# A norm between two layers done token tile by token tile in a held order, latent rows copied out of PSUM, and two attention heads taken two to a step

## The chip, the cores and the metric

The kernel runs on one core of a Trainium2 chip. The metric is the device time of one execution in microseconds, the median of several runs. Engines are named as the profile names them: PE (TensorE matmul), PEld (its weight load), DVE (VectorE), ACT (ScalarE), POOL (GpSimd) and SP (SyncE, which issues nearly all DMA transfers).

## The reference

256 tokens of width 2048 go through one gated-MLP layer and one attention layer, all in float32. Cut to what matters:

```
x:   256 tokens x 2048          c: a vector of 2048 (conditioning)
mod  = silu(c) @ W_ada + b      # shift, scale, gate (2048 each) for layer a, layer b; shift, scale for the shared keys

# layer a (gated MLP)
h        = rms_norm(x, g0) * (1 + scale_a) + shift_a
u, v, z  = split(h @ w_in)                       # 2048 -> 3 x 4096
v        = layer_norm(gelu(v));  mixed = per group of 256 columns: tril(w_s) @ v + b_s
x1       = x + gate_a * ((gelu(u) * mixed * silu(z)) @ w_out)          # 4096 -> 2048

# shared keys and values, from x1
c_kv, k_r = split(mod_k(rms_norm(x1)) @ w_dkv)   # 512 and 64 columns
c_kv = rms_norm(c_kv);  k_nope, v = heads(c_kv @ w_ukv);  k_rope = rope(rms_norm(k_r))

# layer b (attention, 16 heads)
h        = rms_norm(x1, g1) * (1 + scale_b) + shift_b
c_q, z   = split(h @ w_in)                       # 512 and 2048 columns
q        = heads(rms_norm(c_q) @ w_uq);  o = causal_attention(q, k, v)
out      = x1 + gate_b * ((o * silu(z)) @ w_out)
```

## The kernel before

**Tiling.** The tokens are two tiles of 128 (`t` = 0, 1). A product is a `Block`: 1024 output columns (two PSUM banks of 512 for each tile, `pm` in the profile), over k-steps of 256 rows of the weight. Each k-step streams 1 MB of weights (`load`, tile `raw`). A float32 product is made of three reduced-precision ones: ACT casts the weights to `hi` (L192), DVE takes the remainder `lo` (L197), the activations are split likewise (`hh`/`hl` in the input blocks, `shi`/`slo` in the first out-projection and the dkv block, `gh`/`gl` for the second norm, `ybh`/`ybl` in the last projection), and PE does hi·hi, lo·hi and hi·lo: 24 matmuls of 128x512 a k-step for the two tiles and two banks (L392).

**Background work.** The modulation vectors need 128 further loads of 1 MB (`araw`, L214) and one DVE product each (L222; the last gate `ga1` in four pieces of 512, L222 `part`). They are spread over the k-steps by quotas: `AQ` a step in layer a, `BQ` in the z blocks, `OQ` in the last projection. `STOP = 14` ends them at k-step 14 of the second a_w_out block. `raw` and `araw` share a ring of four buffers, `hi` and `lo` rings hold two k-steps, and large intermediates sit in 13 slots of `big`.

**Order.** Work is written as items with a `prepare` (load and split), a `compute` (matmuls) and a `post`; `drive` (L396 on) prepares the next item before it computes the present one, and pops one function from the list `later` (an attention head, a transposed latent row) after each. SP's order is the written one. On PE, ACT and DVE a scheduler orders what is ready, except where `nc.keep("order")` pins an engine's written order and where `behind(...)` puts one instruction after another.

**Second norm.** The second a_w_out block (k-steps 0 to 15) has `TAIL = 1`: its last k-step is done tile by tile, each tile followed by its two residuals (L707 product with the gate, L708 sum, DVE) and, for each, `norm1.chunk`: the sum of squares (L173, ACT) and four transposes (L293, PE; copied to `zT` by ACT, L295). Then `early1(t)` takes the reciprocal root (L186, L167 on DVE, L168 on POOL), spreads it over the partitions with a PE transpose (`px<-ident,rs`, L323), scales the first `EARLY = 4` rows of `zT` (L332, DVE) and makes the first four h (L340 and L341 on ACT, L350 on DVE: tiles `h`, `gh`, `gl`). `late1` does the other twelve for both tiles together. The z block (`b_w_z`, matmuls `pm<-hi,gh` and so on) reads them.

**Latent rows.** After the dkv block and after the q block, `latent_row` sums the squares straight from PSUM (L173), takes the reciprocal root and scales from PSUM to `cn` (L800). Only then are the banks free for the next block.

**Out-projection.** The two b_w_out blocks start while the last heads are still in `later`; each half of the last gate is collected at k-step `GATE1` = 3 (first block) and 4 (second block), and loads whatever `ga1` products are still missing.

**Start.** `opening` splits the first weights, makes the first two h, and runs two pairs of modulation products on DVE in a pinned order (`nc.keep("order")`, all under L69).

Of the kernel before, what the change touches and what calls it, by code (L numbers as in the profile page):

```python
# [10 lines left out]
F32R = mybir.dt.float32r  # L11
# [34 lines left out]
STOP = 14  # L46
# [69 lines left out]
def trunk_kernel(ctx: ExitStack, tc: tile.TileContext, a: dict, out: bass.AP):  # L116
# [74 lines left out]
    def split(src, hi, lo):  # L191
        nc.scalar.copy(hi, src)  # L192
        with behind(chain.pop(0) if chain and queue[0] else None):
            rest(src, hi, lo)
# [8 lines left out]
    hold, queue, chain = [None], [False], []  # L203
# [75 lines left out]
    class Norm:  # L279
# [10 lines left out]
        def flip(self, t, q):  # L290
            p = bank("px")
            for j in range(4):
                nc.tensor.transpose(p[:, j * P:(j + 1) * P], self.xt[t][:, (q * 4 + j) * P:(q * 4 + j + 1) * P], ident)  # L293
            dst = self.ts[q // 2].rearrange("p (k t) -> p k t", t=S)[:, (q % 2) * 4:(q % 2) * 4 + 4, t * P:(t + 1) * P]
            nc.scalar.copy(dst, p.rearrange("p (k t) -> p k t", t=P))  # L295
# [41 lines left out]
        def high(self, n, k, hi, t0=0, t1=S):  # L337
# [5 lines left out]

        def part(self, k, dst):

            src = self.ts[k // 8][:, (k % 8) * S:(k % 8 + 1) * S]
            nc.scalar.activation(dst, src, AF.Identity, scale=ada["sc0"].col[:, k:k + 1], bias=ada["sh0"].col[:, k:k + 1])
# [35 lines left out]
    def mms(ps, t, lh, wt, widths, first, last, apart=False):  # L383

        offs = [sum(widths[:i]) for i in range(len(widths))]
        for some in ([[i] for i in range(len(widths))] if apart else [range(len(widths))]):
# [11 lines left out]
    def drive(items):  # L398
# [5 lines left out]
        while nxt:  # L404
# [3 lines left out]
            if nxt and not late:  # L408
                queue[0] = True
                ready = nxt[0]()  # L410
                queue[0] = False
            cur[1](got)
            if nxt and late:
                queue[0] = True
                ready = nxt[0]()
                queue[0] = False
# [4 lines left out]
    class Block:  # L421
# [21 lines left out]
        def close(self, evac=None, t=None):  # L443
            for t_ in range(NT) if t is None else (t,):
                for i, wd in enumerate(self.widths):
# [4 lines left out]
        def items(self, quota=0.0, tail=0, after=None, before=None, then=None, start=0, stop=99, at_step={}):  # L450
            n = self.nkk - tail
            for kk in range(n):
# [8 lines left out]
            if tail:  # L461
# [8 lines left out]
                def comp(got):  # L470
                    for t in range(NT):
# [3 lines left out]
                        if after:  # L475
                            after(t)
                def post():
                    if then:
                        then()
                    bg(quota * tail if n < stop else 0.0)  # L480
                yield (prep, comp, post, "late") if then else (prep, comp, post)
# [93 lines left out]
    def opening(b):  # L575
# [12 lines left out]
        split(raw[:, 1:2, :], *wt[1])  # L588
# [489 lines left out]
```

## Time and profile before

| what | value |
|---|---|
| time, median of 3 runs | 1129.98 us (1128.75 to 1131.89) |
| the profiled execution's own time | 1134.16 us |
| its span | 1132.5 us, mean granted PE clock 0.995 |
| busy share PE / PEld / DVE / ACT / POOL | 97% / 81% / 84% / 55% / 5% |
| matmul and transpose instructions | 5128 |
| DMA | 340.41 MB, mean 301 GB/s |

The page is to be read from two sides. Its shares say that PE works nearly all the time. Its list of waits says where PE does not, and the windows and the timeline say how each such place runs and at which granted clock (`PEclk`). The profiled execution lay 4.2 us above the median of the runs.

### The profile page before, as it was taken

The numbers are of one execution on the slowest core, as the hardware profiler recorded it, in microseconds if no ns is written. First come the engines' busy times: TensorE is split into PE (matmuls) and PEld (weight loads), VectorE is DVE, ScalarE is ACT, GpSimd is POOL, SyncE is SP. The second block draws the span as 40 slices with busy tenths as digits, with TensorE's granted clock in tenths as the row PEclk, the third lists the DMA queues.
The fourth block names the chain that finished last, engine by engine and source line by source line (L and its number), as shares of the span: only waits on it lengthen the run. The fifth ranks groups of instructions, "written<-read, shape, count | busy, mean of one in ns | idle before, by whom it ended". The sixth has DMA issues, their size and how long they took to land.

```text
span 1132.5 us, 14354 instructions
## 1 busy us (share of the span) xinstructions
PE 1097.4 (97%) x5128; PEld 912.6 (81%) x5128; DVE 950.4 (84%) x1375; ACT 620.3 (55%) x1146; POOL 62.2 (5%) x79
## 2 busy tenths in 40 slices
PE   5999999999999999999999999989999999999998
PEld 4877788887888887888888888868889788898876
DVE  5889899988997887897798899869877658779985
ACT  6844444456754435435354455457737579885322
POOL 1000000000310000000000000000000024220000
PEclk9999999999999999999999999999999999999999
DMA  9987889887998988989979989967896645245893
GB/s 384 353 342 291 329 330 364 343 311 282 351 338 300 367 327 318 386 305 342 343 297 353 375 335 375 353 234 288 318 341 224 221 152 194 105 166 215 301 343 128
DMA packets 52328, 340.41 MB, mean 301 GB/s; under 512 B 5888, under 2 KB 6304, under 8 KB 13984
## 3 DMA queue, kind: packets, MB, share of 16 engines
q1 hardware_dynamic: 50400, 335.29, 78.7%
q0 software_dynamic: 704, 2.11, 0.6%
q10 hardware_dynamic: 1152, 2.10, 0.5%
q8 instruction: 40, 0.66, 0.2%
q14 instruction: 32, 0.26, 0.1%
HBM read 337.36 MB, written 2.11 MB: 300 GB/s over the span
## 4 chain that ended last, share of the span: by engine, by line
PE 73%; DVE 11%; DMA 9%; ACT 3%; issue 3%; POOL 0%; SPq 0%; DVEq 0%; ACTq 0%; POOLq 0%
PE pm L392 60%; DMA araw<-in_ada_wT 5%; PE pk L392 4%; DVE lo L197 4%; DVE araw L222 3%; PE pq L392 2%; DMA araw<-in_kv_ada_wT 2%; DMA raw<-in_b_w_z 1%; PE pmix L663 1%; ACT hi L192 1%; PE pS L967 1%; PE pS L968 1%; DVE v L537 1%; PE pt L670 1%; DVE araw L69 1%
## 5 line engine op out<-in xcount | busy, mean ns | idle before, releaser
L192 ACT CAST hi<-raw 128x1024 fp32r<-128x1024 f32 (+2 forms) x372 | 376.3, 1029 | 358.6 <-PE pm L392 238.8
L197 DVE TENSOR_TENSOR lo<-raw,hi 128x1024 fp32r<-128x1024 f32 (+2 forms) x372 | 436.9, 1195 | 60.5 <-ACT hi L192 58.0
L222 DVE CUSTOM_DVE_ANT_0 araw<-araw,s_b,vec 128x2048 f32<-128x2048 f32 (+1 forms) x124 | 265.6, 2142 | 55.1 <-DMA araw<-in_ada_wT 48.4
L392 PE MATMUL pm<-lo,hh 128*128 128x512 f32 x760 | 245.2, 392 | 3.0 <-DVE lo L197 2.9
L392 PE MATMUL pm<-hi,hl 128*128 128x512 f32 x760 | 243.6, 391 | 0.0
L392 PE MATMUL pm<-hi,hh 128*128 128x512 f32 x760 | 238.2, 393 | 2.6 <-DVE u L537 1.2
L392 PEld LDWEIGHTS pm<-hi,hh 128*128 128x128 f32 x760 | 142.1, 188 | 35.5 <-ACT hi L192 2.2
L392 PEld LDWEIGHTS pm<-lo,hh 128*128 128x128 f32 x760 | 141.6, 188 | 35.3 <-DVE lo L197 6.4
L392 PEld LDWEIGHTS pm<-hi,hl 128*128 128x128 f32 x760 | 142.5, 188 | 29.8
L392 PE MATMUL pm<-lo,shi 128*128 128x512 f32 (+1 forms) x320 | 95.0, 373 | 0.0
L392 PE MATMUL pm<-hi,slo 128*128 128x512 f32 (+1 forms) x320 | 93.4, 371 | 0.0
L392 PE MATMUL pm<-hi,shi 128*128 128x512 f32 (+1 forms) x320 | 91.3, 373 | 0.6 <-ACT hi L192 0.6
L392 PEld LDWEIGHTS pm<-hi,shi 128*128 128x128 f32 x320 | 58.2, 188 | 11.3 <-ACT hi L192 0.9
L392 PEld LDWEIGHTS pm<-lo,shi 128*128 128x128 f32 x320 | 58.2, 188 | 10.1 <-DVE lo L197 0.6
L392 PEld LDWEIGHTS pm<-hi,slo 128*128 128x128 f32 x320 | 58.0, 188 | 10.1
L392 PE MATMUL pm<-hi,gh 128*128 128x512 f32 x160 | 52.3, 400 | 3.5 <-ACT cn L800 2.3
L392 PE MATMUL pm<-lo,gh 128*128 128x512 f32 x160 | 52.8, 397 | 0.0
L392 PE MATMUL pm<-hi,gl 128*128 128x512 f32 x160 | 52.6, 397 | 0.0
L192 ACT CAST shi<-yT 128x512 fp32r<-128x512 f32 x32 | 19.8, 622 | 46.1 <-PE pm L392 46.0
L392 PE MATMUL pm<-hi,ybh 128*128 128x512 f32 x128 | 42.9, 398 | 1.4 <-ACT ybh L192 1.4
L392 PE MATMUL pm<-hi,ybl 128*128 128x512 f32 x128 | 43.1, 399 | 0.0
L392 PE MATMUL pm<-lo,ybh 128*128 128x512 f32 x128 | 43.0, 394 | 0.0
(207 smaller groups left out, 1282.3 us busy)
## 6 DMA issues: line engine op xcount, KB each, us to landing
araw<-in_ada_wT SPq DMA_DIRECT2D x96, 1024.0 KB, 6.6
raw<-in_a_w_in SPq DMA_DIRECT2D x96, 1024.0 KB, 6.7
raw<-in_a_w_out SPq DMA_DIRECT2D x32, 1024.0 KB, 6.9
araw<-in_kv_ada_wT SPq DMA_DIRECT2D x32, 1024.0 KB, 7.3
raw<-in_b_w_z SPq DMA_DIRECT2D x16, 1024.0 KB, 7.5
raw<-in_b_w_out SPq DMA_DIRECT2D x16, 1024.0 KB, 6.1
raw<-in_kv_w_ukv SPq DMA_DIRECT2D x8, 1024.0 KB, 4.9
raw<-in_b_w_uq SPq DMA_DIRECT2D x8, 768.0 KB, 4.5
```

Source lines behind the costliest of these rows:

```text
L69: ins = f(*args, **kw)
L192: nc.scalar.copy(hi, src)
L197: nc.vector.tensor_tensor(out=lo, in0=src, in1=hi.bitcast(F32), op=ALU.subtract)
L222: nc.vector.tensor_tensor_reduce(out=t[:, c], in0=t[:, c], in1=s_b[:, c], scale=1.0, scalar=acc, op0=ALU.mult, op1=ALU.add, accum_out=dst)
L392: nc.tensor.matmul(ps[i][:, :widths[i]], lhsT=lt, rhs=rhs[:, offs[i]:offs[i] + widths[i]], start=(first and c == 0 and which == 0 and rhs ...
L537: nc.vector.tensor_tensor(out=p, in0=ps, in1=p, op=ALU.add)
L663: nc.tensor.matmul(pmix[:, j * 256:(j + 1) * 256], lhsT=wsh["T"][:, g, :], rhs=piece(vt[i], t, n)[:, j * 256:(j + 1) * 256], start=True, s ...
L670: nc.tensor.transpose(pt[:, j * P:(j + 1) * P], y[:, j * P:(j + 1) * P], ident)
L967: nc.tensor.matmul(pS[:, c0:c1], lhsT=qT[:, j, t * P:(t + 1) * P], rhs=kT[:, j, 0:nk], start=True, stop=False)
L968: nc.tensor.matmul(pS[:, c0:c1], lhsT=qrT[:, t * P:(t + 1) * P], rhs=krT[:, j, 0:nk], start=False, stop=True)
```

## The change

Four places of the program change; the arithmetic is the same but for the place at which a latent row is scaled.

1. `passage()` replaces the last two k-steps of the second a_w_out block and the first two of the first z block by one item whose order is pinned on PE, ACT and DVE: tile 0 through k-steps 14 and 15, its residuals, sums and reciprocal root; tile 1 through both, bank by bank, with the work of tile 0's norm among it; then z k-steps 0 and 1 for tile 0, with tile 1's norm among them; then the same for tile 1. z k-step 0's weights are split into two slots of `big` (`zw`), and sums of squares come right behind each residual, transposes later. `early1`, `chunk`, `finish`, `chain` and `queue` go. `STOP` is 13, and `late1` moves the place behind which background products are held (`hold[0]`) every four h.
2. `latent_row` copies the PSUM banks to SBUF with DVE; a new `normalise` then sums, and scales the copy. The dkv block does its last k-step tile by tile.
3. `onward` pops one more item of `later` at k-steps 1 and 2 of the first b_w_out block.
4. In `opening`, the second `lo` comes behind the second pair of modulation products.

```diff
-STOP = 14
+STOP = 13
...
-        def chunk(self, t, q):
-            self.sums(t, q)
-            self.flip(t, q)
-
-        def finish(self, t):
-
+        def rstd(self, t):
             if self.rb is None:
                 self.rb = const.tile([P, S], F32, name=self.name + "rb")
-            r = rstd_sum(self.st[t], 4, D)
+            return rstd_sum(self.st[t], 4, D)
+
+        def spread(self, r):
+
             p = bank("px")
             nc.tensor.transpose(p[:, :P], r.broadcast_to([P, P]), ident)
             return p[:, :P]
...
         norm0.low(h, h0.at(0, 0), h0.at(1, 0))
-        split(raw[:, 1:2, :], *wt[1])
+        nc.scalar.copy(wt[1][0], raw[:, 1:2, :])
         ada["sh0"].step()
         ada["sc0"].step()
+        rest(raw[:, 1:2, :], *wt[1])
...
-                norm1.chunk(t, 2 * i + n)
+                norm1.sums(t, 2 * i + n)
+                if i == 0:
+                    norm1.flip(t, n)
...
-            yield from b.items(AQ, tail=TAIL, after=early1 if i else None, then=late1 if i else None, before=fetch, stop=STOP if i else 99)
+            if i == 0:
+                yield from b.items(AQ, tail=TAIL, before=fetch)
+            else:
+                yield from b.items(AQ, tail=2, stop=STOP, bare=True)
+                at["z"] = z_block(0)
+                yield passage(b, at["z"], fetch)
+
+    def passage(b, z, fetch):
...
+            nc.keep("order")
+            for c in range(2):
+                s = slot(f"zw{c}", F32R)
+                z0.append((s[:, 0:NB], s[:, NB:2 * NB]))
+                split(begin[:, c], *z0[c])
+            mms(b.ps[0], 0, la, wa, wd, False, False)
+            mms(b.ps[0], 0, lb, wb, wd, False, True, True)
+            b.close(t=0)
+            mms(b.ps[1], 1, la, wa, wd, False, False)
+            mms(b.ps[1], 1, lb, wb, wd, False, True, [0])
+            r = norm1.rstd(0)
+            hi, lo = ([wsp.tile([P, 1, NB], F32R, tag=g, name=g) for _ in range(2)] for g in ("hi", "lo"))
+            z1 = [(hi[c][:, 0, :], lo[c][:, 0, :]) for c in range(2)]
+            for c in range(2):
+                nc.scalar.copy(hi[c], raw[:, c:c + 1, :])
+            rest(raw[:, 0:1, :], hi[0], lo[0])
+            rb = norm1.spread(r)
+            norm1.scale(0, EARLY, 0, P, rb)
+            mms(b.ps[1], 1, lb, wb, wd, False, True, [1])
+            p = norm1.turn(0, 2)
...
+            z.ps = [[bank("pm", "mm") for _ in z.widths] for _ in range(NT)]
+            mms(z.ps[0], 0, z.lhs(0), z0, wd, True, False)
+            p = norm1.turn(0, 3)
+            norm1.flipped(0, 3, p)
+            mms(z.ps[0], 0, z.lhs(1), z1[:1], wd, False, False)
+            r = norm1.rstd(1)
+            rest(raw[:, 1:2, :], hi[1], lo[1])
+            rb = norm1.spread(r)
+            norm1.scale(0, EARLY, P, S, rb)
+            mms(z.ps[0], 0, lambda c, w: z.lhs(1)(1, w), z1[1:], wd, False, False)
+            p = norm1.turn(1, 2)
+            for k0 in range(0, EARLY, 2):
+                hs = [norm1.high("1", k, at1[k][0], P, S) for k in (k0, k0 + 1)]
+                for k in (k0, k0 + 1):
+                    hold[0] = norm1.low(hs[k - k0], *at1[k])
+            norm1.keep(1, rb)
+            norm1.flipped(1, 2, p)
+            for j, w in enumerate((z0, z1)):
+                mms(z.ps[1], 1, z.lhs(j), w, wd, j == 0, False)
+            nc.keep("behind")
+            norm1.flip(1, 3)
+        return prep, comp, late1, "late"
...
-            norm1.h("1", k, h1.at(0, k), h1.at(1, k))
+            low = norm1.h("1", k, h1.at(0, k), h1.at(1, k))
+            if k % 4 == 1:
+                hold[0] = low
...
-        r = rms_rstd(pieces)
         cn = scratch([P, R], "cn", "b")
         o = 0
         for p in pieces:
             n = p.shape[-1]
-            nc.scalar.activation(cn[:, o:o + n], p, AF.Identity, scale=r)
+            nc.vector.tensor_copy(cn[:, o:o + n], p)
             o += n
         return cn
+
+    def normalise(row):
+        nc.scalar.activation(row, row, AF.Identity, scale=rms_rstd([row]))
...
+        def onward():
+            if later:
+                later.popleft()()
...
-            yield from b.items(OQ, tail=1, at_step={GATE1[i]: lambda i=i: gate1.half(i)})
+            yield from b.items(OQ, tail=1, at_step={GATE1[i]: lambda i=i: gate1.half(i), **({1: onward, 2: onward} if i == 0 else {})})
```

On PE, at the end of the second a_w_out block, the program had this order (`shi`, `slo`: the block's activations; `x_0_185`, `x_1_186`: the residual rows of tile 0 and 1; `rs`: a tile's reciprocal root):

```order
L392 MATMUL pm<-hi,slo 128x512
L293 MATMUL px<-ident,x_0_185 128x128 x8
L323 MATMUL px<-ident,rs_5839 128x128
L293 MATMUL px<-ident,x_1_186 128x128 x8
L392 MATMUL pm<-hi,gh_5844 128x512 x2
L392 MATMUL pm<-lo,gh_5844 128x512 x2
L323 MATMUL px<-ident,rs_5901 128x128
L392 MATMUL pm<-hi,gl_5846 128x512 x2
```

It now has this one (what `passage` issues carries the line of the pinned order, L69):

```order
L69 MATMUL px<-ident,rs_5844 128x128
L69 MATMUL pm<-hi,shi 128x512
...
L69 MATMUL px<-ident,x_0_185 128x128 x4
L69 MATMUL pm<-zw_5784,gh_5780 128x512 x4
L69 MATMUL pm<-zw_5784,gl_5782 128x512 x2
L69 MATMUL pm<-zw_5787,gh_5780 128x512 x4
L69 MATMUL pm<-zw_5787,gl_5782 128x512 x2
L69 MATMUL px<-ident,x_0_185 128x128 x4
L69 MATMUL pm<-hi,gh_5780 128x512 x2
L69 MATMUL pm<-lo,gh_5780 128x512 x2
L69 MATMUL pm<-hi,gl_5782 128x512 x2
L69 MATMUL px<-ident,rs_5925 128x128
```

Tile 0's spread moved ahead of the last bank of tile 1, tile 1's behind three quarters of tile 0's share of the two z steps, and the transposes of the residual rows are no longer together. On DVE, a little later, when the other h are made, the order was:

```order
L332 TENSOR_TENSOR zT_188<-zT_188,zrb 128x1024 x2
L222 ISA araw,col_sck<-araw,s_b,vec 128x2048
L222 ISA col_sck 128x1
L197 TENSOR_TENSOR lo<-raw,hi 128x1024
L350 TENSOR_TENSOR gl_5846<-h,gh_5844 128x256 x2
L197 TENSOR_TENSOR lo<-raw,hi 128x1024
L226 SCALAR_TENSOR_TENSOR col_sck<-col_sck,vec 128x1
L197 TENSOR_TENSOR lo<-raw,hi 128x1024 x2
L350 TENSOR_TENSOR gl_5846<-h,gh_5844 128x256 x2
L222 ISA araw,col_shk<-araw,s_b,vec 128x2048
```

and is now:

```order
L353 TENSOR_TENSOR gl_5783<-h,gh_5781 128x256 x2
L221 ISA araw,col_shk<-araw,s_b,vec 128x2048
L221 ISA col_shk 128x1
L221 ISA araw,col_sck<-araw,s_b,vec 128x2048
L221 ISA col_sck 128x1
L221 ISA araw,col_shk<-araw,s_b,vec 128x2048
L221 ISA col_shk 128x1
L353 TENSOR_TENSOR gl_5783<-h,gh_5781 128x256 x2
L196 TENSOR_TENSOR lo<-raw,hi 128x1024
```

Three background products that stood one by one between remainders now stand in a row, behind most of the h. After the dkv block, ACT scaled the latent rows straight out of PSUM:

```order
L173 ACTIVATE sq,ss_6960<-pm 128x288
L173 ACTIVATE sq,ss_6960<-pm 128x224
L192 CAST hi<-raw 128x1024
L800 ACTIVATE cn<-pm,rs_6968 128x288
L800 ACTIVATE cn<-pm,rs_6968 128x224
L173 ACTIVATE sq,ss_6974<-pm 128x64
L843 ACTIVATE kn<-pm,rs_6978 128x64
```

and now DVE takes them out of PSUM, behind two remainders of the next block's weights:

```order
L196 TENSOR_TENSOR lo<-raw,hi 128x1024 x2
L870 COPY cn<-pm 128x288
L870 COPY cn<-pm 128x224
L914 COPY kn<-pm 128x64
L870 COPY cn<-pm 128x288
L870 COPY cn<-pm 128x224
L914 COPY kn<-pm 128x64
L196 TENSOR_TENSOR lo<-raw,hi 128x1024 x2
L167 TENSOR_SCALAR rs_6945<-ss_6942 128x1
```

The root and the scale moved behind the copies. On SP, in the first b_w_out block, the loads around the first half of the last gate were in this order:

```order
L214 DMA araw<-in_ada_wT 128x2048
L367 DMA raw<-in_b_w_out 128x2048
L214 DMA araw<-in_ada_wT 128x2048 x3
L367 DMA raw<-in_b_w_out 128x2048
L214 DMA araw<-in_ada_wT 128x2048
```

and are now in this:

```order
L213 DMA araw<-in_ada_wT 128x2048
L370 DMA raw<-in_b_w_out 128x2048
L213 DMA araw<-in_ada_wT 128x2048 x4
L370 DMA raw<-in_b_w_out 128x2048
L213 DMA araw<-in_ada_wT 128x2048
```

One more modulation load stands ahead of that block's sixth weight load.

More of the change, by code (lines that the diff above doesn't have):

```diff
@@ L192, in split @@
         nc.scalar.copy(hi, src)
-        with behind(chain.pop(0) if chain and queue[0] else None):
-            rest(src, hi, lo)
+        rest(src, hi, lo)
     def rest(src, hi, lo):
@@ L448, in close, with items @@
                 self.ps = None
-        def items(self, quota=0.0, tail=0, after=None, before=None, then=None, start=0, stop=99, at_step={}):
+        def items(self, quota=0.0, tail=0, before=None, start=0, stop=99, skip=0, bare=False, at_step={}):
             n = self.nkk - tail
-            for kk in range(n):
+            for kk in range(skip, n):
                 def post(kk=kk):
@@ L859, in ev_q @@
         cn = latent_row([ps])
+        normalise(cn)
         if t == 0:
```

81 lines of the change are left out of this document (48 added, 33 removed).

## The prediction

> **What bounds the kernel now.** I read the page's shares first, then PE's list of waits, then windows and the timeline round each wait that the change touches.
>
> ```profile
> PE 1097.4 (97%) x5128; PEld 912.6 (81%) x5128; DVE 950.4 (84%) x1375; ACT 620.3 (55%) x1146; POOL 62.2 (5%) x79
> ```
>
> PE works 97% of the span, and the change takes no matmul away. So nothing can be won but what PE loses: some 35 us of idle time (1132.5 - 1097.4), and what its slow stretches add. The list of PE's waits (total, times, longest) names the losses. These are the ones in reach:
>
> ```profile
> PE pm L392 <- ACT cn L800: 2.3, 1, 2.3
> PE px L323 <- POOL rs L168: 2.1, 1, 2.1
> PE pm L392 <- ACT ybh L192: 1.4, 1, 1.4
> PE pm L69 <- ACT hh L69: 1.0, 1, 1.0
> PE pm L392 <- ACT gh L341: 0.8, 1, 0.8
> ```
>
> They sum to 7.6 us, but two of these waits cost more than their length. The windows (length, then busy time of PE, PEld, DVE, ACT, POOL, then granted PE clock, DMA share, GB/s) show it:
>
> ```profile
> 755.60:763.00 7.40, 3.64 (x18) 2.62 (x17) 5.67 (x13) 6.73 (x18) 0.81 (x2) 0.74 0.02 4
> 763.00:767.40 4.40, 4.39 (x14) 3.45 (x15) 3.85 (x7) 3.15 (x11) 0.30 (x1) 0.65 0.24 80
> 767.40:785.00 17.60, 17.60 (x79) 14.53 (x78) 17.60 (x23) 12.63 (x24) 0.00 (x0) 1.00 0.74 282
> 881.60:885.60 4.00, 3.97 (x11) 3.12 (x12) 1.11 (x5) 1.91 (x9) 1.10 (x2) 0.57 0.71 279
> 1075.00:1095.00 20.00, 18.60 (x83) 14.99 (x82) 19.85 (x37) 5.82 (x7) 0.00 (x0) 1.00 0.91 337
> ```
>
> After the norm's wait (755.6 to 763) and after the latent row's (before 881.6) PE is "busy" at a clock of 0.65 and 0.57: 14 and 11 instructions in 4 us, where the third row does 79 in 17.6 us, 0.223 us each. Behind the 1.4 us wait for `ybh` (last row) the clock stayed 1.00.
>
> **The passage into the z block.** The timeline there (start, length, engine):
>
> ```profile
> 667.23 0.60 PE L293 MATMUL px<-ident,x 128*128 128x128 f32 x4
> 667.58 0.71 PE L392 MATMUL pm<-lo,shi 128*128 128x512 f32 x2
> ...
> 755.41 0.39 PE L392 MATMUL pm<-hi,slo 128*128 128x512 f32 x1
> 757.03 0.69 DVE L707 TENSOR_TENSOR x<-pm,gate 128x512 f32<-128x512 f32 x1
> 757.63 1.28 DVE L708 TENSOR_TENSOR x<-x,xr 128x512 f32<-128x512 f32 x2
> 758.15 0.63 ACT L173 ACTIVATE sq<-x 128x512 f32<-128x512 f32 x1
> 758.90 0.16 DVE L186 TENSOR_REDUCE ss<-st 128x1 f32<-128x4 f32 x1
> 759.40 0.56 POOL L168 TENSOR_TENSOR rs<-rs,nhalf 128x1 f32<-128x1 f32 x1 [125.87 <-DVE rs L167]
> 760.01 0.48 PE L323 MATMUL px<-ident,rs 128*128 128x128 f32 x1 [2.12 <-POOL rs L168]
> 760.53 0.69 DVE L332 TENSOR_TENSOR zT<-zT,px 128x512 f32<-128x512 f32 x1 [1.28 <-PE px L323]
> 761.41 0.88 ACT L340 ACTIVATE h<-zT,col_sh,col_sc 128x128 f32<-128x128 f32 x2
> 762.66 0.30 ACT L341 CAST gh<-h 128x128 fp32r<-128x128 f32 x1
> 763.01 1.22 PE L392 MATMUL pm<-hi,gh 128*128 128x512 f32 x2 [0.81 <-ACT gh L341]
> 767.38 0.62 PE L392 MATMUL pm<-hi,gh 128*128 128x512 f32 x2
> ```
>
> The group of the weights' casts (busy, mean ns):
>
> ```profile
> L192 ACT CAST hi<-raw 128x1024 fp32r<-128x1024 f32 (+2 forms) x372 | 376.3, 1029 | 358.6 <-PE pm L392 238.8
> ```
>
> What it costs now: the last a_w_out matmul starts at 755.41 and takes its slot of 0.23, so from 755.64 to the first full-rate matmul at 767.38 are 11.74 us. In them PE does 16 transposes (four cost 0.35 at full clock, 667.23 to 667.58: 1.40), two spreads (0.17) and 12 matmuls (12 x 0.223 = 2.7): 4.2. The loss is 7.5 us.
>
> What it will cost: I walk along the held orders with these durations, from PE's start on tile 0's k-step 14. A tile has 12 matmuls of 0.223 a k-step. Tile 0's bank 0 is done at 4.0, bank 1 at 5.4. The two residual pairs (0.69 + 0.64 each) end at 6.8, the sum at 7.6, reduction and root at 8.8. PE comes to tile 0's spread behind tile 1's bank 0, at 9.4: no wait. The rows scale from 9.9 to 10.6; `gh` is there at about 11.3; PE, past bank 1 and four transposes (10.7 + 0.35), waits 0.2. Here the move covers tile 0's chain with 12 to 18 matmuls of tile 1. Tile 1 is covered less: DVE does its residuals behind tile 0's scale and among four `gl`, to 13.7; ACT's sums queue behind tile 0's h and end near 16; the root is there at 16.8, PE at 15.8: 1.0 wait and 0.4 until the order runs on. Behind this spread stand six z matmuls that need nothing of it, so PE's wait is pure loss. Then z k-step 2 needs `gh` of k = 4. ACT has tile 1's four h and their casts (0.44 + 0.30 each), two copies and two casts of 1.03 ahead of it, some 6 us from 18.0, then its own; PE's 30 matmuls and eight transposes end near 24.5: 1.3 wait. Last, three background products stand in a row on DVE (2.35 each by the start's row below, 7.1 us) where they stood apart, ahead of the remainder for z k-step 6: 0.5 there and 0.55 at the y block's second step. Total 3.9, gain 3.6. Bounds: if all these slips hide in the two k-steps that PE is prepared ahead, 0.6 is left and the gain is 7; if ACT's and DVE's queues slip by twice as much, 7.8 is lost and the gain is none.
>
> The clock decides whether such waits count once or more. In this trace 1.40 us of waiting left it at 1.00, and 2.12 and 2.28 us cost half the clock for some 3 us, 1.5 us of work. My longest wait is 1.3. [...] By the rows, a wait of mine that passes 2 us costs 1.5 more, which gives 1123.8.
>
> **The z and y blocks.** While PE waits at the norm, the transfers stand still: 4 GB/s in the first window row, the ring being full. Later ACT's casts wait for weights:
>
> ```profile
> ACT hi L192 <- DMA raw<-in_b_w_z: 16.7, 4, 5.1
> 820.00:855.00 35.00, 34.36 (x158) 28.52 (x156) 28.90 (x40) 12.24 (x15) 0.00 (x0) 1.00 0.91 331
> ```
>
> The window has PE losing 0.64 us there. In the new order the first z weights leave the ring ahead of the residuals, so loads go on. Between 0 (it is covered anyway, or comes elsewhere) and 1.1 (that, and as much again of the small waits) I take 0.5.
>
> **The latent rows.**
>
> ```profile
> 878.66 0.69 PE L392 MATMUL pm<-hi,slo 128*128 128x288 f32 x4
> 878.87 1.23 DVE L197 TENSOR_TENSOR lo<-raw,hi 128x1024 fp32r<-128x1024 f32 x1 [0.37 <-ACT hi L192]
> 881.08 0.84 ACT L800 ACTIVATE cn<-pm,rs 128x288 f32<-128x288 f32 x2 [0.32 <-POOL rs L168]
> 881.63 0.50 PE L392 MATMUL pm<-hi,gh 128*128 128x512 f32 x1 [2.28 <-ACT cn L800]
> 885.62 0.39 PE L392 MATMUL pm<-hi,gh 128*128 128x512 f32 x1
> L987 DVE COPY pts<-pT 128x384 f32<-128x384 f32 x14 | 7.7, 552 | 0.2 <-PE pT L985 0.2
> L904 DVE COPY pair<-pk 128x256 f32<-128x256 f32 x8 | 3.3, 417 | 0.0
> ```
>
> From about 879.20 (the last four in 0.13 steps) to 885.62 are 6.42 us for 9 matmuls and two transposes, 2.2 at full clock: a loss of 4.2. The new copies of 288, 224 and 64 columns are bounded by the two PSUM copies shown; on the line through them they take 0.45, 0.38 and 0.21. Tile 0's banks are done 1.6 us ahead of tile 1's (12 x 0.133), so its copies hide unless DVE is inside a remainder of 1.23: then they end up to 1.7 late. Gain between 2.5 and 4.2; I take 3.6, nearer the hidden end since only one of the two remainders can be late. The sum, root and scale of the copy come later on ACT, hidden by the 8-step q block that follows; without that cover, 2.2 us at the first transposed row.
>
> **The start.**
>
> ```profile
> 20.54 2.35 DVE L69 CUSTOM_DVE_ANT_0 araw<-araw,s_b,vec 128x2048 f32<-128x2048 f32 x1
> 23.92 1.14 PE L293 MATMUL px<-ident,x 128*128 128x128 f32 x8 [0.24 <-ACT xT L295]
> 26.04 0.73 PE L69 MATMUL pm<-hi,hh 128*128 128x512 f32 x2 [0.98 <-ACT hh L69]
> ```
>
> The chain is two products (from 20.54), the column, `hh`, PE. One remainder of 1.22 ahead of it goes behind: PE could start 1.2 earlier, but its transposes end at 25.06, so 0.98 at most, and the remainder now is due at PE's second group. Between 0 and 0.98 I take 0.8.
>
> **The last projection.**
>
> ```profile
> 1095.00:1105.00 10.00, 10.00 (x46) 8.29 (x45) 7.15 (x17) 3.27 (x4) 0.00 (x0) 1.00 0.96 353
> L222 DVE CUSTOM_DVE_ANT_0 araw<-araw,s_b,part 128x512 f32<-128x512 f32 x39 | 28.8, 745 | 0.1
> ```
>
> Two heads come a step early, and the wait of 1.4 for `ybh` goes. What is late next: `STOP` and the background order leave one more gate product here, 4 x 0.745 = 3.0 us on a DVE that has 0.15 us free in the 20 us to 1095 (row above), and 1 MB (3.1 us at 337 GB/s) among transfers that are 0.91 to 0.96 busy, ahead of the sixth weight load. Between -1.4 (all hidden; PE loses nothing in 1095 to 1105) and +2.5 I take +0.8, the middle, a little up for the full DVE.
>
> **Sum.** -3.6 - 0.5 - 3.6 - 0.8 + 0.8 = -7.7 us. It was made against one execution of 1134.16 us, 4.2 above the median of 1129.98; those 4.2 are not in these places' reach, so I put the difference on the median: 1122.3. A measurement here tells about 0.3% (3.4 us) from no change.
>
> **Rivals.**
> - *The passage gives nothing.* Its loss only moves, to z k-steps 2 to 6 (the 7.8 above). For it: DVE is busy 17.60 of 17.60 in the row from 767.4, so work put off has no free place. Against: 3 us of that row's DVE work is now ahead of it. Time: 1122.3 + 3.6 = 1125.9.
> - *The latent wait stays.* Copies on DVE queue behind remainders, and the wait is only renamed, clock included. For: the order has two remainders ahead of the copies. Against: they are prepared a step ahead. Time: 1122.3 + 3.6 = 1125.9; with a passage half as good, 1127.7.
> - *The last projection gives it back.* 3 us of DVE and 3.1 us of DMA both on the path, and the `ybh` wait still there: +6.1 in place of +0.8, 1127.6.
> - *Slower: the held order exposes both chains.* PE now stands at a spread that it must not pass. Row to end now, from tile 0's last residual at 757.0 to 763.01, the chain is 6.0 us; if each tile's is waited for in full, and the clock halves twice (1.5 each), the loss is 15.0 instead of 7.5. With the other terms, +7.5 - 4.1 = +3.4: 1133.4. It decides from a passage loss of some 15 us on; the walk has 3.9, and 18 matmuls (4.1 us) stand before each spread, which speaks against it.
>
> **How the numbers follow.** Forecast 0.62, with its own range 1118.5 to 1126; passage gives nothing 0.15; latent wait stays 0.08; given back at the end 0.08; slower 0.07. All terms at their good ends would give 1116.5; the low end is 1117.0. The high end takes in the three middle rivals: 1127.8. Faster by over 0.3% (below 1126.6): nearly all of the forecast, 0.60, and two thirds of the first two rivals, 0.15, so 0.75; slower: half of the last rival and 0.02 of the one before, 0.06; the rest, 0.19, within.
>
> **What would show it.** Right: no wait at `px<-rs` for tile 0, about 1 us at tile 1's; `PEclk` 1.00 through both places; no row PE <- `cn`; casts waiting less for `in_b_w_z`; `hh` wait near 0.2; no `ybh` wait. Wrong: clock near 0.5 behind the first spread; DVE remainders as the releaser all along z k-steps 2 to 7; a wait in the second b_w_out block.

## The result, and the profile after

The changed kernel takes 1139.7 us (median of 7 runs) against 1131.4 us for the kernel before: a ratio of 1.0068, 95% interval 1.0050 to 1.0087. It is slower; I had forecast 1122.3 and a range to 1127.8. Times are medians over fast runs; one slow run, of 1585 us in the kernel with the pops alone, is left out. The profiled execution took 1137.71 us, its span 1136.0 us: 3.6 us above the profiled execution of before (1134.16), where the medians lie 8.3 apart. So what the traces show below, place by place, is of two single executions, and 4.8 us of the loss stand in neither. First the page's shares and PE's list of waits after (total, times, longest), to be held against those of before:

```profile
PE 1098.1 (97%) x5128; PEld 911.2 (80%) x5128; DVE 954.4 (84%) x1381; ACT 620.1 (55%) x1140; POOL 60.2 (5%) x79
```

```profile
PE pm L395 <- DVE res L705: 5.4, 1, 5.4
PE px L69 <- POOL rs L168: 1.1, 1, 1.1
PE pm L395 <- ACT ybh L192: 0.9, 1, 0.9
PE pm L395 <- ACT gh L349: 0.8, 1, 0.8
PE pm L69 <- ACT gh L69: 0.5, 1, 0.5
PE pm L69 <- ACT hh L69: 0.2, 1, 0.2
```

The waits that the change was to take away are gone or smaller: none for `cn`, 1.1 for `rs` instead of 2.1, `hh` 0.2 instead of 1.0, `ybh` 0.9 instead of 1.4. One wait of 5.4 us is new, and is longer than all that went: PE stands before a b_w_out matmul until DVE has read a PSUM bank for a residual (`res`). It stands at the second b_w_out block, where I had named a wait as a sign of being wrong. Up to the first b_w_out matmul the changed kernel is 6.1 us ahead (1012.24 us against 1018.38). From there to PE's last matmul it needs 118.3 us instead of 108.6: 9.7 us lost in the last projection. The windows there, first two of before, then two of after (length, busy time of PE, PEld, DVE, ACT, POOL, PE clock, DMA share, GB/s):

```profile
1072.00:1082.00 10.00, 8.60 (x43) 6.80 (x42) 9.83 (x20) 2.58 (x3) 0.00 (x0) 1.00 0.97 383
1082.00:1092.00 10.00, 10.00 (x45) 8.26 (x45) 9.88 (x20) 4.01 (x4) 0.00 (x0) 1.00 0.79 288
```

```profile
1072.00:1082.00 10.00, 5.72 (x24) 4.05 (x22) 4.76 (x11) 1.99 (x2) 0.57 (x1) 1.00 0.87 341
1082.00:1092.00 10.00, 8.02 (x24) 6.40 (x25) 8.76 (x15) 0.00 (x0) 0.00 (x0) 0.66 0.49 159
```

After, 48 PE instructions run in the 20 us in which before 88 ran; the clock is 0.66 behind the wait. Forty instructions less at 0.22 us each are 9 us: nearly all of the 9.7 is here. What PE waits for is the last gate's first half. Its chain in the timeline, before:

```profile
1065.03 0.27 PE L272 MATMUL px<-ident,col_ga 128*8 128x128 f32 x1
1065.88 0.57 POOL L276 DMA_DIRECT2D gd<-grow  x1 [38.97 <-ACT grow L274]
1071.23 0.56 POOL L277 DMA_DIRECT2D gate<-gd  x1 [4.77 <-DMA gd<-grow]
1080.74 0.69 DVE L707 TENSOR_TENSOR res<-pm,gate 128x512 f32<-128x512 f32 x1
```

and after:

```profile
1068.66 0.27 PE L271 MATMUL px<-ident,col_ga 128*8 128x128 f32 x1
1069.52 0.57 POOL L275 DMA_DIRECT2D gd<-grow  x1 [48.66 <-ACT grow L273]
1075.64 0.57 POOL L276 DMA_DIRECT2D gate<-gd  x1 [5.54 <-DMA gd<-grow]
1083.24 1.29 DVE L705 TENSOR_TENSOR res<-pm,gate 128x512 f32<-128x512 f32 x2 [6.40 <-DMA gate<-gd]
1083.98 0.80 PE L395 MATMUL pm<-hi,ybh 128*128 128x512 f32 x1 [5.41 <-DVE res L705]
```

The gate's columns are transposed on PE, copied, written out (`gd`), and read back spread over the partitions (`gate`), 12.1 us from the transpose to the rows' landing before (the last transfer took 5.9) and 14.5 after (7.5). The transpose comes 46.6 us into the last projection before, and 56.4 us into it after, though the eight products that it needs were complete 14 and 19 us earlier (1051.3 and 1050.0). In PE's order it stands behind 131 b_w_out matmuls before and behind 168 after; 37 matmuls more at 0.227 are 8.4 us.

### The profile page after: what moved, and what is told of

It is laid out like the page before. It is cut to its first block, busy times and chain, and to the rows that moved or that the text cites. A ratio compares the mean times of both kernels' runs of the same rounds, so it can differ in the third digit from the quotient of the medians.

```text
span 1136.0 us, 14351 instructions
## 1 busy us (share of the span) xinstructions
PE 1098.1 (97%) x5128; PEld 911.2 (80%) x5128; DVE 954.4 (84%) x1381; ACT 620.1 (55%) x1140; POOL 60.2 (5%) x79
## 4 chain that ended last, share of the span: by engine, by line
PE 73%; DVE 10%; DMA 9%; ACT 4%; issue 4%; POOL 0%; SPq 0%; DVEq 0%; ACTq 0%; POOLq 0%
PE pm L395 62%; DMA araw<-in_ada_wT 6%; DVE lo L196 3%; PE pk L395 3%; DVE araw L221 3%; PE pq L395 1%; PE pmix L661 1%; ACT hi L192 1%; PE pm L69 1%; DVE araw L69 1%; DMA lnb<-in_a_ln_b 1%; PE pS L1041 1%; PE pS L1042 1%; DMA gate<-gd 1%; DMA x<-in_x 1%
## 5 line engine op out<-in xcount | busy, mean ns | idle before, releaser
L192 ACT CAST hi<-raw 128x1024 fp32r<-128x1024 f32 (+2 forms) x366 | 369.5, 1028 | 363.3 <-PE pm L395 232.0
L196 DVE TENSOR_TENSOR lo<-raw,hi 128x1024 fp32r<-128x1024 f32 (+2 forms) x366 | 429.8, 1192 | 79.4 <-ACT hi L192 77.4
L395 PE MATMUL pm<-lo,shi 128*128 128x512 f32 (+1 forms) x304 | 89.8, 373 | 1.3 <-DVE lo L196 1.3
L395 PE MATMUL pm<-hi,slo 128*128 128x512 f32 (+1 forms) x304 | 89.4, 370 | 0.0
L395 PE MATMUL pm<-hi,shi 128*128 128x512 f32 (+1 forms) x304 | 85.7, 371 | 0.0
L395 PEld LDWEIGHTS pm<-lo,shi 128*128 128x128 f32 x304 | 55.0, 188 | 11.6 <-DVE lo L196 2.8
L395 PEld LDWEIGHTS pm<-hi,shi 128*128 128x128 f32 x304 | 55.2, 188 | 9.6
L395 PE MATMUL pm<-lo,gh 128*128 128x512 f32 x144 | 47.5, 391 | 0.3 <-DVE lo L196 0.3
L395 PE MATMUL pm<-hi,gl 128*128 128x512 f32 x144 | 47.1, 390 | 0.0
L395 PE MATMUL pm<-hi,gh 128*128 128x512 f32 x144 | 46.2, 392 | 0.8 <-ACT gh L349 0.8
```

The lines of the kernel that those rows point to most:

```text
L196: nc.vector.tensor_tensor(out=lo, in0=src, in1=hi.bitcast(F32), op=ALU.subtract)
L395: nc.tensor.matmul(ps[i][:, :widths[i]], lhsT=lt, rhs=rhs[:, offs[i]:offs[i] + widths[i]], start=(first and c == 0 and which == 0 and rhs ...
```

## The experiments

**The theories.** Theory 1: the early pops move the gate. `half` takes a PSUM bank from the same ring of four as the attention heads, in the order in which the program is written. Before, three pops stand ahead of it; with `onward` five do, so its transpose comes behind two heads more. (The ring and the order are read from the program.) Theory 2: the gate product and the 1 MB load that `STOP = 13` moves into this stage are the cost. Four kernels tell them apart.

The changed kernel without the pops:

```diff
-at_step={GATE1[i]: lambda i=i: gate1.half(i), **({1: onward, 2: onward} if i == 0 else {})}
+at_step={GATE1[i]: lambda i=i: gate1.half(i)}
```

> The changed kernel without the two extra pops of heads in the first b_w_out block; all else stays. Theory 1 (the gate's transpose has been put behind the heads that are popped early: its PSUM bank comes from the same ring of four as theirs, so it stands 168 b_w_out matmuls into the stage on PE instead of 131): without the pops it stands at 137, 31 matmuls or 7 us earlier; the gate rows land ahead of the first block's end, the 5.4 us wait for the residual and the slow clock behind it go, and the time falls by 8 us from the changed kernel's 1139.7, to some 1131 - 8 + 1 for the wait on ybh that comes back: 1126 to 1132, at or below the kernel before. Theory 2 (the one gate product and 1 MB load more in that stage are the cost): no change, 1138 to 1141, and the wait for the gate stays over 3 us.

Measured: 1128.3 us, ratio to before 0.9967 (0.9945 to 0.9989). The transpose stands at 48.0 us into the stage, the wait for `res` is gone, and the two windows are full again:

```profile
1072.00:1082.00 10.00, 8.90 (x39) 7.01 (x39) 9.96 (x20) 2.00 (x2) 0.00 (x0) 1.00 1.01 389
1082.00:1092.00 10.00, 10.00 (x46) 8.29 (x45) 8.59 (x17) 2.00 (x2) 0.00 (x0) 1.00 0.98 317
```

Undoing two pops turns a kernel 0.7% slower than before into one 0.3% faster. Its last projection takes 110.6 us, 2.0 more than before. Next, the other part undone (`STOP = 14`), the pops kept:

> The changed kernel with STOP back at 14: one gate product and one 1 MB load fewer in the last projection, with the two early pops kept. Theory 1: on PE the gate's transpose still stands late, at 154 matmuls instead of 168 (before: 131); the rows land 3 us earlier than in the changed kernel, so a wait of about 2 us stays, less of the slow clock: 1132 to 1137. Theory 2 (the product and the load are the whole cost): no wait for the gate is left and the time is 1123 to 1129.

Measured: 1133.7 us, 1.0023 (1.0005 to 1.0042). The wait stays, 5.2 us and not 2:

```profile
PE pm L395 <- DVE res L705: 5.2, 1, 5.2
```

```profile
1069.48 0.56 POOL L276 DMA_DIRECT2D gate<-gd  x1 [4.95 <-DMA gd<-grow]
1078.47 1.89 DVE L705 TENSOR_TENSOR res<-pm,gate 128x512 f32<-128x512 f32 x3 [4.18 <-DMA gate<-gd]
```

`STOP` alone does not cure it: the total is as theory 1 had it, the wait longer. The 3 us that I had not counted are in the chain's last transfer: issued at 1069.48, landed at 1078.38, 8.9 us instead of the 5.9 of before. In all four kernels that have the `res` wait this transfer took 7.5 to 9.1 us, in the kernel before 5.9. Weights stream beside it (the DMA total while it ran was 320 GB/s before, 315 in the changed kernel); whether they are the reason no run separates. In this trace the last projection takes 116.9 us to the last matmul, 8.3 more than before. Theory 2 alone falls. The pops added to the kernel before, nothing else:

> The kernel before with the two early pops alone. Theory 1: the gate's transpose moves from 131 to 154 matmuls into the stage, 5 us later; the rows land about 1 to 2 us after the first block's end, so a wait of PE for the residual appears and the 1.4 us for ybh goes: 0 to 3 us slower than before. Theory 2: the ybh wait goes and nothing else comes: 1 to 1.5 us faster.

Measured: 1138.7 us, 1.0059 (1.0037 to 1.0082), with the wait

```profile
PE pm L392 <- DVE res L707: 4.2, 1, 4.2
```

The direction is theory 1's, the size was not: I had 0 to 3 us and it is 7 (here the last transfer took 8.2 us). The `ybh` wait of 1.4 us, which the pops were to remove, is there still.

In the fourth the gate does without PE, bank and copy:

```diff
-            p = bank("px")
-            nc.tensor.transpose(p[0:8, 0:P], self.ada.col[:, 8 * h:8 * h + 8], ident)
...
-            nc.gpsimd.dma_start(d.rearrange("o (k p) -> (o k) p", p=P), r)
+            nc.gpsimd.dma_start(d.rearrange("o (k p) -> p (o k)", p=P), self.ada.col[:, 8 * h:8 * h + 8])
```

> The changed kernel, with both early pops and STOP = 13, but the first half of the last gate is written to memory straight from its column tile by one transfer of 128 x 8 single values, without the PE transpose, the PSUM bank and the copy. Theory 1: the columns are complete at 1050 us in the trace, 18 us ahead of the transpose; so the rows land by 1070 even if the transfer of single values takes 10 us, and the wait of 5.4 us with its slow clock goes: 1128 to 1133. Theory 2: the load on DVE and the transfers is what it was, and the time stays at 1137 to 1142.

Measured: 1135.3 us, 1.0043 (1.0022 to 1.0063): between the two theories' times, and above the 1133 of theory 1. The wait for `res` on the gate is gone, as theory 1 said, but with the transfer of 1024 single values a new cost came:

```profile
1051.90 0.96 POOL L272 DMA_DIRECT2D gd<-col_ga  x1 [29.48 <-DVE col_ga L221]
1064.73 0.57 POOL L279 DMA_DIRECT2D gate<-gd  x1 [11.87 <-DMA gd<-col_ga]
```

```profile
1053.00:1063.00 10.00, 10.00 (x56) 8.53 (x55) 5.78 (x17) 0.00 (x0) 0.00 (x0) 1.00 1.04 181
```

```profile
ACT hi L192 <- DMA raw<-in_b_w_out: 14.4, 3, 10.8
```

It takes 12.3 us to land; from 1053 to 1063 us the transfer engines are full (share 1.04) at 181 GB/s, and ACT waits up to 10.8 us for weights (the third row: ACT's waits from 1050 to 1070 us), where its longest such wait in the same 20 us of the changed kernel is 4.3. Waits of PE for heads and `ybh` follow (2.5 for `szb`, a head's output; 2.0 for `ybh`; 1.8 for `pr`, a head's softmax), and the stage takes 117.9 us. With the transpose gone the gate no longer holds PE, but this way of writing it is of no use as a remedy.

**Is it the place, or the pops?** Of these, the kernels with the wait had pops and a late gate together. Two further edits separate them: pops with an early gate, and a late gate without pops. First, the pops stay and the gate goes ahead of them:

```diff
-at_step={GATE1[i]: lambda i=i: gate1.half(i), **({1: onward, 2: onward} if i == 0 else {})}
+at_step={1: lambda: (gate1.half(0), onward()), 2: onward} if i == 0 else {GATE1[i]: lambda i=i: gate1.half(i)}
```

> The changed kernel with the first half of the last gate collected at k-step 1 of the first b_w_out block, ahead of the early pop there, instead of at k-step 3 behind five pops; both early pops and STOP = 13 stay. On PE the gate's transpose then stands 88 matmuls into the stage instead of 168; six gate loads stand in a row ahead of the fourth weight load. Theory 1 (the late place of the gate's chain is the cost of the changed kernel): the rows land some 10 us ahead of the first block's end, no wait for the residual, 1127 to 1133. Rival (DVE with the heads and the extra product is the bound, and the gate only shows it): the wait comes back as one for a head or for weights, and the time stays at 1135 to 1141.

Measured: 1128.5 us, 0.9977 (0.9959 to 0.9995), no wait for `res`. With the gate at k-step 2, behind three pops:

> The changed kernel with the gate's first half at k-step 2 behind three pops, STOP = 13. The transpose stands 144 matmuls into the last projection, between the places that gave no wait (131, 137) and those that gave one (154: 5.2 and 4.2 us, 168: 5.4 us). Theory 1 as a matter of degree: 7 matmuls or 1.6 us behind the 137 whose rows came about 2 us early, so a wait of 0 to 1 us, no slow clock: 1128 to 1132. If instead the pops themselves cost the time: 1135 and more.

Measured: 1132.3 us, 1.0017 (0.9995 to 1.0038): no wait for `res`, but waits for `ybh` (2.3) and `szb` (1.4 in this stage), 113.4 us to the last matmul. That is just above the range that I gave; the wait for the gate is gone, but not all of the time. The other edit is in the kernel before, one number changed:

```diff
-GATE1 = (3, 4)
+GATE1 = (4, 4)
```

> The kernel before with one number changed: the first half of the last gate is collected at k-step 4 of the first b_w_out block instead of 3. No extra pops, no product more, no other edit. On PE the gate's transpose stands 152 matmuls into the last projection instead of 131, as far back as with the early pops (154). If the place of the gate's chain alone costs the time: a wait of PE for the residual of 3 to 5 us, the last projection at 113 to 116 us instead of 108.6 to PE's last matmul, 1135 to 1139. If the pops had cost it in another way (heads crowding DVE): no wait for the residual and within 2 us of the kernel before.

Measured: 1144.5 us, 1.0095 (1.0062 to 1.0128), as much as the whole change lost or more (the intervals overlap). PE's wait, and the windows round it:

```profile
PE pm L392 <- DVE res L707: 6.4, 1, 6.4
```

```profile
1080.00:1090.00 10.00, 5.77 (x24) 4.35 (x24) 7.59 (x14) 2.35 (x3) 0.57 (x1) 0.96 0.99 375
1090.00:1100.00 10.00, 7.41 (x26) 6.03 (x27) 9.51 (x21) 0.00 (x0) 0.00 (x0) 0.70 0.79 278
```

That settles it: a late place of the gate's chain brings the wait and the slow clock by itself, without pops and without a product more. The wait and the stage, 116.9 us, are longer than I had said; the last transfer took 9.1 us here. Of the 11.1 us by which this profiled execution exceeds that of before, 8.3 are in the last projection. At the last spatial mix it was already 4.6 us behind, where the two programs are still the same (it regains 1.8 between): five kernels with the same order on PE up to there reach it between 603.9 and 612.8 us. So single executions are better compared stage by stage than by their totals.

The order from early to late, by matmuls ahead of the transpose, with the stage's length to PE's last matmul, over all kernels that transpose the first half on PE: 88: 109.0 and 111.0; 96: 112.2; 131 (before and three more): 108.6 to 109.2; 137: 110.0 and 110.6; 144: 113.4; 152 (the last kernel): 116.9; 154: 114.6 and 116.9; 168 (the change): 118.3. The `res` wait is there from 152 on and at none before it. The pops, which all of 88, 96 and 144 have, earn nothing even with the gate early: none of these is below 108.6. The moved product shows too. With `STOP = 13` and neither pops nor a late gate the stage takes 110.0 and 110.6 us, with 14 it takes 108.6 to 109.2; and from the first key matmul to the first b_w_out matmul it is 113.0 to 113.1 us in all seven kernels with 13 and 112.0 to 112.1 in all eight with 14. So `STOP = 13` costs some 2 us in these two stretches; the medians without the pops, 1128.3 against 1127.0 below, point the same way.

**The other parts one by one.** Each is put into the kernel before. The latent rows alone:

```diff
-            nc.scalar.activation(cn[:, o:o + n], p, AF.Identity, scale=r)
+            nc.vector.tensor_copy(cn[:, o:o + n], p)
...
-... ev_dkv).items(),
+... ev_dkv).items(tail=1),
```

> The kernel before with the latent rows alone changed: copies out of PSUM by DVE, sums and scale in SBUF, the dkv block's last k-step tile by tile. The prediction's term was 3.6 us; the two traces differ by 5.3 us from the first dkv matmul to the first key matmul (53.9 and 48.5). If all of that is this edit's: 1126 to 1128, no wait for cn, PE's clock 1.00 there. If part of it came from the place in time (transfers further ahead after the passage): 1128 to 1130.

Measured: 1128.2 us, 0.9975 (0.9956 to 0.9993), 3 us. From the first dkv to the first key matmul it takes 49.8 us, against 53.9 before and 48.5 in the changed kernel. In its timeline DVE comes to the copies behind a remainder, and PE waits for the copies instead of the scale:

```profile
876.62 1.23 DVE L197 TENSOR_TENSOR lo<-raw,hi 128x1024 fp32r<-128x1024 f32 x1 [0.36 <-ACT hi L192]
877.76 0.75 DVE L799 COPY cn<-pm 128x288 f32<-128x288 f32 x2
878.27 0.50 PE L392 MATMUL pm<-hi,gh 128*128 128x512 f32 x1 [1.18 <-DVE cn L799]
```

In the changed kernel the same copies meet no remainder, and PE's matmul has no wait:

```profile
875.68 0.75 DVE L870 COPY cn<-pm 128x288 f32<-128x288 f32 x2
876.28 0.47 PE L395 MATMUL pm<-hi,gh 128*128 128x512 f32 x1
```

The passage alone, with `STOP = 13`:

> The kernel before with the passage alone changed, with STOP = 13 which belongs to it; opening, latent rows and pops as before. The prediction's terms were 3.6 and 0.5 us, and the traces differ by 3.1 us between the fifth u block and the first dkv matmul. If this holds and the one gate product more in the last projection costs under 1 us: 1127 to 1130. If that product gives back what the passage wins: 1130 to 1133.

Measured: 1130.2 us, 0.9994 (0.9974 to 1.0014): not told from no change. Its profiled execution, the fastest of its twelve runs, does show the local gain, 241.1 us from the last spatial mix to the first dkv matmul, where five kernels with the old passage have 243.8 to 244.7. But of ten kernels with the new passage only two have 241.1 or 241.2; the others have 242.9 to 246.0. In each of these eight the trace has a wait: in the three with `STOP` at 14, tile 0's spread waits 2.2 us; in four of the seven with 13, PE waits 1.3 to 2.0 us at the y block for `szb` (here the z block's result, which must leave its banks); the eighth is the kernel of the last test in this part. And `STOP = 13` takes back some 2 us behind the passage, as said above.

The opening alone (the second remainder behind the second pair of products):

> The kernel before with the opening alone changed (the second remainder behind the second pair of products). The prediction's term was 0.8 us. The trace of the changed kernel has PE 1.1 us earlier at the second pair of h, and waits of PE for remainders between 28 and 120 us that are 1.3 us longer. If the gain holds: 1130 to 1131, ratio 0.999; if it is given back at these remainders: no difference, 0.9985 to 1.0015.

Measured: 1132.5 us, 1.0007 (0.9989 to 1.0025). No gain is shown; one of 0.8 us would lie within the interval.

I tried one cause of the y block's late weights. The transfers slacken at 775 to 785 us, I supposed because three products in a row keep their buffers; DMA share 0.86 before, 0.53 with the new passage (second: the passage alone):

```profile
775.00:785.00 10.00, 10.00 (x46) 8.22 (x45) 10.00 (x15) 6.97 (x13) 0.00 (x0) 1.00 0.86 321
```

```profile
775.00:785.00 10.00, 10.00 (x46) 8.29 (x45) 9.18 (x12) 7.48 (x15) 0.00 (x0) 1.00 0.53 184
```

So in the kernel with the gate at k-step 1 I let the products go one by one again:

```diff
-            low = norm1.h("1", k, h1.at(0, k), h1.at(1, k))
-            if k % 4 == 1:
-                hold[0] = low
+            norm1.h("1", k, h1.at(0, k), h1.at(1, k))
```

> The kernel with the gate's half at k-step 1 (1128.5 us), and the background products held only behind the passage, no longer behind every fourth of the later h: they stand one by one on DVE among the remainders again instead of three in a row. Theory (three products in a row keep their buffers, so the transfers rest at 775 to 785 us and the y block's weights come late): transfers go on in that stretch, the wait for szb of 1.7 us in the y block goes, and the stretch from the fifth u block to the first dkv matmul falls from 242.8 to 241 or less; 1126 to 1128. Rival (a product ahead of a remainder or of an h costs PE as much at z k-steps 2 to 5): the same 1128 to 1130, with waits for gl or lo there.

Measured: 1134.4 us, 1.0028 (1.0012 to 1.0045). The rival's kind of wait came, and more of it than its 1128 to 1130: PE waits for an h and for its remainder.

```profile
PE pm L395 <- ACT gh L349: 2.5, 1, 2.5
PE pm L395 <- DVE gl L353: 2.3, 1, 2.3
```

The transfers do go on (share 0.76 at 775 to 785 us, 0.49 in the kernel without this edit) and the `szb` wait is gone, so the theory had that part right. But the stretch to dkv takes 246.0 us instead of 242.9: the row of three products was the lesser evil.

**A version that beats both.** The three other parts without the pops, `STOP = 14`:

> The changed kernel without the early pops and with STOP back at 14: the last projection is then as in the kernel before, and the passage, the latent rows and the opening stay changed. If these three gain what the traces show up to the start of the last projection (6.1 us earlier), and nothing of it is lost behind, the time is 1124 to 1127 (ratio 0.993 to 0.996) and below the variant without the pops alone by 1 to 3 us. If the last projection is bound by something that does not start earlier (transfers), 1128 to 1131.

Measured: 1127.0 us, 0.9954 (0.9940 to 0.9968): the fastest of all. With pops and the gate at k-step 1, also at `STOP = 14`:

> The changed kernel with the gate's first half collected at k-step 1 of the first b_w_out block, ahead of the early pop there, and STOP back at 14: the candidate that should keep all that the change wins. The gate's transpose stands 96 matmuls into the last projection, five gate loads in a row instead of six. If the gate's place is what cost the time and the product more costs 1 to 2 us (the variants without pops: 1128.3 against 1127.0): 1124 to 1127, ratio 0.993 to 0.997. If the early pops are worth nothing beside the gate: the same as without them, 1127.

Measured: 1132.8 us, 1.0031 (1.0007 to 1.0055), a miss. The gate is early (34 us into the stage), but PE waits 2.8 us for `ybh` and 1.2 for `ybl` in the last projection. Its profiled execution took 1128.95 us, 3.8 below its median, so the trace does not show what the longer runs lose. Why five gate loads in a row do worse here than six with `STOP = 13` stays open.

## Why the prediction was wrong

Point by point, by its own steps.

- *The last projection: the step that failed.* I put it at +0.8 us, between -1.4 and +2.5; it measured +9.7 between the two traces. I priced the edit by the work that it brings (a gate product, a megabyte) and wrote that "the wait of 1.4 for `ybh` goes". The part that I priced was about right: without the pops `STOP = 13` costs the stage 1.4 us (110.0 against 108.6, and 110.6 against 109.2). What I put at nothing, and even on the credit side, was the pops. I did not follow what they are moved past: the collecting of the gate at k-step 3, its PSUM bank, and two transfers in series behind it. The order after had the transpose at 168 matmuls instead of 131, and the rows of before give its chain 12 us to the landing (two issues 5.35 us apart and 5.9 us for the last transfer), with 3.6 us to spare ahead of the first residual at 1080.74. Worked out there, 37 matmuls later by 8.4 us put the rows some 5 us behind that residual, an estimate from these rows; the last transfer then took 1.6 us longer as well. The result was a PE wait of 5.4 us with a slow clock behind it. Even the `ybh` wait stayed: 0.9 us, and 1.4 us with the pops alone.
- *The rival "given back at the end"* named the right stage with a wrong mechanism, and gave 1127.6, so its price was 6.1 where 9.7 was needed. What PE waited for was one small chain in a late place, and its last transfer took 7.5 us instead of 5.9, for a reason that no run separates.
- *The passage: right in itself, not worth what I said.* The walk gave waits of 0.2 at tile 0's h, 1.0 at tile 1's spread and 1.3 at z k-step 2, and a full clock. The timeline after has 0.5, 1.1 and 0.8, and a clock of 1.00:

```profile
755.72 0.32 PE L69 MATMUL px<-ident,rs 128*128 128x128 f32 x1
758.34 1.20 PE L69 MATMUL pm<-zw,gh 128*128 128x512 f32 x4 [0.49 <-ACT gh L69]
764.33 0.32 PE L69 MATMUL px<-ident,rs 128*128 128x128 f32 x1 [1.13 <-POOL rs L168]
773.25 0.72 PE L395 MATMUL pm<-hi,gh 128*128 128x512 f32 x2 [0.79 <-ACT gh L349]
```

  To the dkv block 3.1 us were won in this execution, against 4.1 (3.6 and 0.5) forecast. Over the runs of the passage alone it is 1.2 us, not told from nothing. The y block behind it, which I had put on the credit side, takes some of it back in four of the seven traces with `STOP = 13`, and ACT's casts, which were to wait less for `in_b_w_z`, wait 18.7 us instead of 16.7. `STOP = 13` costs some 2 us more behind it. The rival "the passage gives nothing" is nearer than the forecast.
- *The latent rows: right.* 3.6 forecast, 3.2 measured alone. The gain depends on where DVE stands in its remainders, as I wrote. The rival that the wait is only renamed has a part in it: alone, 1.2 of the 2.3 us stay, for DVE's copies, but little else is lost: from the first dkv to the first key matmul that kernel takes 49.8 us, the changed one 48.5, and the clock of the latter is 1.00 from 874 to 878 us.
- *The start: mechanism right, gain not shown.* The `hh` wait fell from 1.0 to 0.2, but the remainders behind it came later, and PE waited for such between 28 and 120 us 1.6 us in all instead of 0.9. With the opening alone those waits stayed at 0.9 and the `hh` wait went, and still the ratio was 1.0007; 0.8 us cannot be told there.
- *The slower rival* (both norm chains exposed) did not occur: tile 0's spread has no wait at all. That the time still came out slower is not its merit.
- *The clock.* I made a fixed price of 1.5 us out of two waits of one trace; behind the same 2.28 us the clock was 0.57 over 4 us in one kernel and 1.00 in another (last section).
- *The range.* The terms at their good ends add up to -14.7 us, 1115.3, and not the 1116.5 that I wrote; it moves nothing else.

Sum: without the pops and with `STOP` as it was, the change is worth 4.4 us, where I had 8.5 (7.7 and the 0.8); with the pops and the product moved it became a loss of 8.3. Between those two medians lie 12.7 us; the two profiled executions differ by 10.0, of which 9.1 are in the last projection (118.3 against 109.2). The rest stays open.

## What to carry to other kernels

When an edit pulls work forward in a program whose buffers go round in written order, list what the work is moved past, and follow each of these to its end: here a small transpose at the head of a chain of two transfers had 3.6 us of slack, and 21 matmuls of delay stopped PE for 6.4 us, with the clock at 0.70 over the 10 us from 1090. Price a moved piece by the chain behind what it overtakes, not by its own duration. And a gain of some us at one stage, as the passage had, counts only if the stages behind it do not take it back: look there for new waits.

## What the runs showed of the hardware

The same wait does not always slow PE's clock. Four kernels run the latent rows in the old way with the same wait of 2.28 us for `cn`. In three the clock then falls over the next 4 us, in the kernel before and the one with the opening alone to 0.57, in the one with the gate at k-step 4 to 0.62; in the one with the pops alone it does not (windows of 4 us from the first matmul behind the wait; the opening alone, then the pops alone):

```profile
879.90:883.90 4.00, 4.00 (x12) 3.13 (x13) 1.04 (x5) 1.91 (x10) 1.10 (x2) 0.57 0.73 270
```

```profile
880.10:884.10 4.00, 3.99 (x18) 3.29 (x19) 1.08 (x5) 1.92 (x9) 1.09 (x2) 1.00 0.78 255
```

Twelve instructions or eighteen in the same 4 us, at the same place behind the same wait: 1.3 us more or less. Other waits say the same: behind 1.99 us for `szb` at 806.19 in the kernel with the gate at k-step 2, matmuls of 128x512 start 0.43 us apart at 807.27, 807.70 and 808.13, but behind 2.10 us for `sz` at 135.16 in the one with the gate at k-step 4 they start 0.23 us apart at 135.50, 135.73 and 135.96, and 2.58 us for `cn` with the passage alone were followed by 1.00. Between the first 30 us and PE's last matmul the kernel before has two stretches of slow clock, 6.83 us (759.21 to 766.04) and 3.41 us (882.09 to 885.50), the changed kernel has one of 6.83 us (1082.76 to 1089.59), all three at 0.50; PE's waits that end in or just ahead of them are 2.12, 2.28 and 5.41 us long. So a price for a slow clock behind a wait of some 2 us is a chance and no constant, which I had made of it.

A transfer of 1024 single values, 4 KB in all, took 12.3 us to land where the one of transposed rows, 4 KB too, took 5.6 in the changed kernel (median of four). In its time, from 1053 to 1063 us, the transfer engines were full (share 1.04) at 181 GB/s, and from 1050 to 1070 us ACT's longest wait for weights of 1 MB was 10.8 us, 4.3 us in the same 20 us of the changed kernel.
